# Sparse-attention loop of a hybrid decoder layer: filler weights' low parts by adding DMA, head outputs summed on VectorE, every key block in two float32r parts, masked 128-row compressed values

## The chip, the cores and the metric

One core of one Trainium2 chip runs the whole program. The metric is device time in microseconds (us) of one execution; lower is better. The time before is the median of three runs.

## What is computed

One decoder layer over 512 tokens of width 1024, in float32: a conditioned RMS norm, three token mixers side by side (a chunked gMLP, an mLSTM and NSA sparse attention), a gated merge, an output projection, a conditioned squared-ReLU MLP and a final norm. The change lies in the attention and in what runs beside it:

```python
sc = einsum('bgrqd,bgcd->bgrqc', qb, k_cmp) * scale - slopes * (tf - cmp_center)
p_c = masked_softmax(sc, cmp_end <= t);   o_cmp = einsum('bgrqc,bgcd->bgrqd', p_c, v_cmp)
o_sel = softmax over the selected blocks of 64 keys (8 of 8 here) @ v_sel
o_win = softmax over the last 512 keys @ v_win
out = gate_c * o_cmp + gate_s * o_sel + gate_w * o_win      # 8 heads of 64, in 2 groups of 4
```

There are 31 compressed positions a group. With 512 tokens the selected blocks are all blocks, so the second and the third branch are both full causal softmaxes, over different keys and values.

## The kernel before, in words

A product in float32 is made of float32r parts: hi is the value rounded to float32r, lo = value - hi, and a*b is hi*hi + hi*lo + lo*hi in PSUM. A function `split` (line 89 on) makes both parts: ScalarE copies the source to hi, then VectorE subtracts. `chunk` (line 105) does it for weights: SyncE loads 128x1024 into `w_raw`, ScalarE makes `w_hi` (L109), VectorE or, with `pool_lo`, GpSimd makes `w_lo` (L110).

The attention (us 114 to 266 of the profile) is a loop written out by hand, in whose order TensorE, ScalarE and VectorE are held. It has 18 steps n of four quarters i. Step n belongs to the pair (head h = n // 2, branch n % 2). A quarter holds, in this order:

- `scores(n, i)`: queries of 128-token block i times all keys up to it (PE L511, L512), then bias and row maximum in one VectorE pass (L513; L516 negates the four maxima after block 3);
- `exps(n-1, ..)`: ScalarE exponentials and row sums of the step before (L521);
- `turn(n-2, i)`: TensorE transposes (L541) of key block i, and their evacuation from PSUM to `pt`. In quarter 0 it comes behind the filler;
- `run(fill, ..)`: some six matmuls of the filler, which computes other projections of the layer (`early_fill`, 12 units of one chunk; L889, L905). At a unit's start it calls `chunk` for the next unit, with `pool_lo`;
- `apply(..)`, three quarters behind its `turn`: values times `pt` into the head's accumulator (L566), ahead of the filler in quarter 0. The first one of a head adds the compressed branch (L558, L559);
- `scale(n-1, ..)` in quarters 2 and 3: VectorE multiplies two rows of scores each by gate / sum (L527, L528, L531). The quarter-0 transposes of the next step need all four.

Key blocks 0 and 1 (512 and 384 query columns) are split into `pt_hi` and `pt_lo` against float32r values `V2` = [hi | lo]; blocks 2 and 3 (256 and 128 columns) stay float32: ScalarE copies them to `pt` (L548), and one float32 matmul multiplies them by `V32` = [v | 0], which runs as two instructions. The compressed values `vc` of a head are 32 of 128 rows; its matmul uses these 32 rows alone. The accumulator has 128 rows: 64 of the hi values, 64 of the lo values. When a head is done, in quarter 2 of the even steps 4 to 18, ScalarE copies both halves (L573); when the second head of a pair is done, GpSimd adds the halves and splits the sum (L581 to L583), and for the last pair VectorE and ScalarE do. GpSimd also makes a head's `bias` (L503) in this stretch. The second group's compressed scores (`cmp_scores(1)`) are worked off in pieces in steps 4 to 7.

Of the kernel before, what the change touches and what calls it, by code (L numbers as in the profile page):

```python
# [24 lines left out]
GELU_A = 0.044715  # L25
ML_SCALE = 128.0 ** -0.5
FILL_AT = (1, 2, 3, 4)
DVE_HI = False
SB_BUFS = 3
PRE_FILL = 16  # L30
LAST_X = (6,)
CONV_POOL = False
# [4 lines left out]
ADA_BUFS = 8  # L37
DVE_LO = ((1, 0), (1, 1), (1, 2), (1, 3))
CMP_AT = ((4, 0), (4, 2), (5, 0), (5, 2), (6, 0), (6, 2), (6, 3), (7, 1))
SPLIT_SB = (0,1)  # L40
SLOPES = [2.0 ** (-(h + 1)) for h in range(8)]


# [17 lines left out]
def trunk_kernel(ctx: ExitStack, tc: tile.TileContext, x, vecs, rows, late_rows, ada1, w_ada,  # L61
# [40 lines left out]
        nc.sync.dma_start(raw[:, :cols], src)  # L102
        return raw[:, :cols]

    def chunk(src, cols=D, pool_lo=False, dve_hi=False):
        raw = load(src, cols)
        hi = stream.tile([P, D], F32R, name="w_hi", tag="hi")[:, :cols]
        lo = stream.tile([P, D], F32R, name="w_lo", tag="lo")[:, :cols]
        V.tensor_copy(hi, raw) if dve_hi else A.copy(hi, raw)  # L109
        (G if pool_lo else V).tensor_tensor(lo, raw, f(hi), op=ALU.subtract)  # L110
        return hi, lo

    def mm3(ps, ah, al, bh, bl, first, last):
# [128 lines left out]
    with tc.manual_schedule(engines={mybir.EngineType.PE}):  # L242
# [6 lines left out]
        for j in range(KD):  # L249
# [7 lines left out]
            for i in range(6):  # L257
# [15 lines left out]
    G.memset(flag, 1.0)  # L273
    G.affine_select(out=flag, in_=flag, pattern=[[0, 1]], compare_op=ALU.is_ge, fill=0.0, base=-31,
                    channel_multiplier=1)
    dmask = const.tile([P, P], F32, name="dmask")
    G.memset(dmask, 0.0)
    G.affine_select(out=dmask, in_=dmask, pattern=[[1, P]], compare_op=ALU.is_ge, fill=-NEG, base=0,
# [104 lines left out]
    def compress(n):  # L383
        hp = bank("S", "hid")
        for m in range(16):
            T.matmul(hp[:, :128], phis[n][:, m].rearrange("p s c -> p (s c)"),
                     wins[n][:, m].rearrange("p s c -> p (s c)"), start=m == 0, stop=m == 15)
        hs = small.tile([64, 64], F32, name="c_hid")
        t1 = small.tile([64, 64], F32, name="c_t1")
        A.copy(t1, hp[64:128, :64])  # L390
        V.tensor_tensor(t1, t1, hp[:64, 64:128], op=ALU.add)
        V.tensor_tensor(hs, t1, hp[:64, :64], op=ALU.add)
        V.tensor_tensor(t1, hs, hs, op=ALU.mult)
        V.tensor_scalar(t1, t1, GELU_A, 1.0, op0=ALU.mult, op1=ALU.add)
        V.tensor_tensor(t1, t1, hs, op=ALU.mult)
        A.activation(t1, t1, AF.Tanh, scale=GELU_C)
        V.scalar_tensor_tensor(t1, t1, 1.0, hs, op0=ALU.add, op1=ALU.mult)
        V.tensor_scalar(hs, t1, 0.5, None, op0=ALU.mult)
        if n == 0:
            kp = bank("S", "kcmp")  # L400
            T.matmul(kp[:, :64], p2[:, 0:128], hs, start=True, stop=True)
            split(kc2[:, :, 0, :], kc2[:, :, 1, :], kp[:, :64].rearrange("p (g c) -> p g c", g=2))
            return
        for g in range(2):
            hr = small.tile([64, 4, 32], F32, name="c_rep")
            V.tensor_copy(hr, hs[:, g * 32:(g + 1) * 32].unsqueeze(1).to_broadcast([64, 4, 32]))
            vp = bank("S", "vcmp")
            T.matmul(vp[:, :64], hr.rearrange("e r c -> e (r c)"), p2[:, 128:192], start=True, stop=True)
            vv = nsa.tile([P, 128], F32R, name=f"vc{g}")
            split(vv[:, 0:64], vv[:, 64:128], vp[:, :64])  # L410
            vc.append(vv)

    windows(0, zt(ZT_NKC, True, "T"), V_PEK)
    windows(1, zt(ZT_NVC, True, "T"), V_PEV)
# [2 lines left out]


    V2 = [page("kv", f"v2_{tb}", F32R).rearrange("p (b g e) -> p b g e", b=2, g=2) for tb in range(NT)]
    V32 = [nsa.tile([P, 2, 2, 128], F32, name=f"v32_{tb}") for tb in range(NT)]  # L420
    mg = const.tile([P, NT, 8], F32, name="mg")
    gate = const.tile([P, NT, 24], F32, name="gate")
    gv3 = gate.rearrange("p t (h b) -> p t h b", b=3)
# [11 lines left out]
                T.matmul(sm[tb][:, :288], hh[k][:, tsl(tb)], wl[:, ws_], start=False, stop=k == KD - 1)  # L435
    for tb in range(NT):
        src = sm[tb][:, 0:256].rearrange("p (b g e) -> p b g e", b=2, g=2)
        V.tensor_copy(V32[tb][:, :, :, 0:64], src)
        G.memset(V32[tb][:, :, :, 64:128], 0.0)
        split(V2[tb][:, :, :, 0:64], V2[tb][:, :, :, 64:128], V32[tb][:, :, :, 0:64])  # L440
        V.tensor_tensor(mg[:, tb, :], sm[tb][:, 256:264], gb, op=ALU.add)
        A.activation(gate[:, tb, :], sm[tb][:, 264:288], AF.Tanh, scale=0.5)
    V.tensor_scalar(gate, gate, 1.0, 0.5, op0=ALU.add, op1=ALU.mult)
# [91 lines left out]
    def turn(n, sb):  # L535

        sb_ = step_[n][0]
        c0 = sb * P
        tp = bank("T", "pT")
        for tb in range(sb, NT):  # L540
            T.transpose(tp[:, tsl(tb)], sb_[:, boff(tb) + c0:boff(tb) + c0 + P], ident)  # L541
        if sb in SPLIT_SB:
            ph, pl = temp(att, "pt_hi", "pt", 8, F32R), temp(att, "pt_lo", "pt", 8, F32R)
            split(ph[:, c0:], pl[:, c0:], tp[:, c0:])
            pts_[n, sb] = (ph, pl)
        else:
            pt = temp(att, "pt", "pt", 8)
            A.copy(pt[:, c0:], tp[:, c0:])  # L548
            pts_[n, sb] = (pt,)

    def apply(n, sb):

        h, br = divmod(n, 2)
        g, r = divmod(h, 4)
        if br == 0 and sb == 0:
            pr = slice(r * 32, r * 32 + 32)
            accs[h] = bank("acc", "pv")
            T.matmul(accs[h], vc[g][pr, :], pc[g][0][pr, :], start=True, stop=False)  # L558
            T.matmul(accs[h], vc[g][pr, :], pc[g][1][pr, :], start=False, stop=False)  # L559
        acc = accs[h]  # L560
        c0 = sb * P
        last = br == 1 and sb == NT - 1
        t = pts_.pop((n, sb))
        vv = (V2 if len(t) == 2 else V32)[sb][:, br, g, :]
        for p_ in t:
            T.matmul(acc[:, c0:], vv, p_[:, c0:], start=False, stop=last and p_ is t[-1])  # L566
        if not last:
            return
        i = h // 2
        if h % 2 == 0:  # L570
            yraw[i] = [temp(att, "y_c", "y_c", 2) for _ in range(2)]
        for part, y in enumerate(yraw[i]):
            A.copy(y[(h % 2) * 64:(h % 2) * 64 + 64, :], acc[part * 64:part * 64 + 64, :])  # L573
        if h % 2 == 1:
            y, y2 = yraw[i]
            ych[i], ycl[i] = page("yc", "yc_hi", F32R), page("yc", "yc_lo", F32R)
            if i == 3:
                V.tensor_tensor(y, y, y2, op=ALU.add)
                split(ych[i], ycl[i], y)
                return  # L580
            G.tensor_tensor(y, y, y2, op=ALU.add)  # L581
            G.tensor_copy(ych[i], y)
            G.tensor_tensor(ycl[i], y, f(ych[i]), op=ALU.subtract)  # L583


    gvr = [None] * 4
# [285 lines left out]
    def early_fill():  # L872

        units = [("t", 0), ("t", 1), ("t", 2), ("t", 3)] + [("z", g) for g in range(4)] + [
            ("t", 4), ("t", 5), ("t", 6), ("t", 7)]

        def prep(u):
            return chunk(w_tok[u[1]] if u[0] == "t" else w_zt[ZT_GU + u[1]], D, True, DVE_HI)

        nxt = prep(units[0])  # L880
        for m, (kind, i) in enumerate(units):
            wh, wl = nxt
            if m + 1 < len(units):
                nxt = prep(units[m + 1])
            if kind == "z":
                ps = bank("mm", "zt")
                mms = [(wh, k, o) for k in range(KD) for o in (hh, hl)] + [(wl, k, hh) for k in range(KD)]
                for n_, (w_, k, o) in enumerate(mms):
                    T.matmul(ps, w_[:, tsl(k)], o[k], start=n_ == 0, stop=n_ == len(mms) - 1)  # L889
                    if n_ % 3 == 2 and n_ < len(mms) - 1:  # L890
                        yield
                gur[i] = page("mr", "gu")
                A.copy(gur[i], ps)
                yield
                continue
            n, c = divmod(i, 2)
            if c == 0:
                ps = [bank("mm", "ztok") for _ in range(2)]

            mms = [(tb, kk, a_, wh) for tb in range(NT) for kk in range(4) for a_ in (hh, hl)]  # L900
            mms += [(tb, kk, hh, wl) for tb in range(NT) for kk in range(4)]
            for n_, (tb, kk, a_, w_) in enumerate(mms):
                k = 4 * c + kk
                o = ps[tb // 2][:, (tb % 2) * 256:(tb % 2) * 256 + 256]
                T.matmul(o, a_[k][:, tsl(tb)], w_[:, kk * 256:(kk + 1) * 256],  # L905
                         start=k == 0 and tb % 2 == 0 and a_ is hh and w_ is wh,
                         stop=k == KD - 1 and tb % 2 == 1 and w_ is wl)
# [468 lines left out]
```

## Time and profile before

| | |
|---|---|
| median of 3 runs | 974.91 us (974.37 to 975.87) |
| the profiled execution | 973.78 us, span 972.0 us |
| TensorE busy | 932.9 us (96%), 4688 matmuls |
| VectorE busy | 618.3 us (64%) |
| ScalarE busy | 404.4 us (42%) |
| GpSimd busy | 194.8 us (20%) |
| DMA | 111.72 MB, 115 GB/s on average |

Matmuls are pipelined, so a row's duration is longer than what it takes from the next one; the distance from start to start is what it costs. A wait is put down to the instruction that came last. Line numbers before are those of the kernel above; in the order of the changed kernel they are its own.

### The profile page before, as it was taken

Reading aid. Unit: us, or ns where it says so; the run is one execution under the profiler, and the core shown is the slowest. Engines: PE = TensorE matmul, PEld = TensorE weight load, DVE = VectorE, ACT = ScalarE, POOL = GpSimd, SP = SyncE. Lnnn points to the kernel's source line nnn. Section 1 sums busy time; section 2 is a strip of 40 time slices with the busy share of each in tenths; the row PEclk is TensorE's granted clock in tenths of the full one; section 3 lists DMA queues with packets and bytes.
Section 4 is the critical chain, followed back from the end, with each engine's and each line's share of the span. In section 5 each row is a group of like instructions: output and inputs, shape, how many; then the busy total and the mean of one; then the engine's idle time right before and its main releaser. Section 6 shows DMA issues by size and latency. Waiting matters only on the chain.

```text
span 972.0 us, 12530 instructions
## 1 busy us (share of the span) xinstructions
PE 932.9 (96%) x4688; PEld 781.5 (80%) x4688; DVE 618.3 (64%) x1186; ACT 404.4 (42%) x789; POOL 194.8 (20%) x130
## 2 busy tenths in 40 slices
PE   8789998998999999999999998999999999999997
PEld 6568996797877888888988887988888888888886
DVE  5977688777389666656688889766424254442435
ACT  4355565665463434444243344544321223432221
POOL 5564442332344123123300003000000000000001
PEclk8799999998999999999999999999999999999999
DMA  8643310110132122222478872364332323223222
GB/s 307 217 132 100 101 45 22 44 45 22 53 112 75 65 86 93 82 87 87 155 237 262 296 255 85 90 183 130 96 99 90 106 89 107 87 89 106 87 87 88
DMA packets 36286, 111.72 MB, mean 115 GB/s; under 512 B 4160, under 2 KB 4352, under 8 KB 36224
## 3 DMA queue, kind: packets, MB, share of 16 engines
q1 hardware_dynamic: 36224, 110.91, 35.1%
q8 instruction: 37, 0.61, 0.3%
q14 instruction: 25, 0.20, 0.1%
HBM read 108.80 MB, written 2.10 MB: 114 GB/s over the span
## 4 chain that ended last, share of the span: by engine, by line
PE 81%; DVE 13%; DMA 2%; issue 2%; ACT 1%; POOL 0%; SPq 0%; POOLq 0%; ACTq 0%
PE tok L1106 7%; PE tok L1105 7%; PE tok L1104 7%; PE m L115 6%; PE m L114 6%; PE m L116 6%; PE zt L120 5%; PE zt L121 5%; PE zt L293 5%; PE ztok L905 4%; PE pv L566 2%; DMA ada_raw<-in_ada 2%; PE up L120 2%; PE up L121 2%; PE up L858 2%
## 5 line engine op out<-in xcount | busy, mean ns | idle before, releaser
L109 ACT CAST w_hi<-w_raw 128x1024 fp32r<-128x1024 f32 (+2 forms) x137 | 141.4, 1033 | 248.7 <-PE tok L1105 97.1
L110 DVE TENSOR_TENSOR w_lo<-w_raw,w_hi 128x1024 fp32r<-128x1024 f32 x84 | 107.4, 1279 | 164.2 <-ACT w_hi L109 157.2
L110 POOL TENSOR_TENSOR w_lo<-w_raw,w_hi 128x1024 fp32r<-128x1024 f32 (+3 forms) x53 | 126.5, 2388 | 252.4 <-ACT w_hi L109 149.7
L120 PE MATMUL zt<-h_hi,w_hi 128*128 128x512 f32 x272 | 107.8, 396 | 0.0
L121 PE MATMUL zt<-h_lo,w_hi 128*128 128x512 f32 x272 | 107.4, 395 | 0.0
L114 PE MATMUL m<-h_hi,w_hi 128*128 128x512 f32 (+1 forms) x272 | 103.8, 382 | 0.0
L115 PE MATMUL m<-h_lo,w_hi 128*128 128x512 f32 (+1 forms) x272 | 103.7, 381 | 0.0
L116 PE MATMUL m<-h_hi,w_lo 128*128 128x512 f32 (+1 forms) x272 | 103.4, 380 | 0.0
L1104 PE MATMUL tok<-w_hi,f_hi 128*128 128x512 f32 (+1 forms) x232 | 88.7, 382 | 0.0
L1105 PE MATMUL tok<-w_hi,f_lo 128*128 128x512 f32 (+1 forms) x232 | 88.7, 382 | 0.0
L1106 PE MATMUL tok<-w_lo,f_hi 128*128 128x512 f32 (+1 forms) x232 | 84.4, 382 | 0.0
L293 PE MATMUL zt<-h_hi,w_lo 128*128 128x512 f32 x272 | 70.1, 393 | 0.0
L1246 POOL TENSOR_TENSOR o_g<-x,gfin 128x512 f32<-128x512 f32 x1 | 1.3, 1293 | 310.7 <-DVE x L1150 310.7
L120 PEld LDWEIGHTS zt<-h_hi,w_hi 128*128 128x128 f32 x272 | 51.4, 189 | 10.8 <-ACT num_lo L787 0.4
L121 PEld LDWEIGHTS zt<-h_lo,w_hi 128*128 128x128 f32 x272 | 51.4, 189 | 10.4
L114 PEld LDWEIGHTS m<-h_hi,w_hi 128*128 128x128 f32 x272 | 51.0, 187 | 10.8
L115 PEld LDWEIGHTS m<-h_lo,w_hi 128*128 128x128 f32 x272 | 51.1, 188 | 10.6
L116 PEld LDWEIGHTS m<-h_hi,w_lo 128*128 128x128 f32 x272 | 51.1, 188 | 10.5
L293 PEld LDWEIGHTS zt<-h_hi,w_lo 128*128 128x128 f32 x272 | 50.8, 188 | 10.5
L1104 PEld LDWEIGHTS tok<-w_hi,f_hi 128*128 128x128 f32 x232 | 43.6, 188 | 8.5
L1105 PEld LDWEIGHTS tok<-w_hi,f_lo 128*128 128x128 f32 x232 | 43.6, 188 | 8.5
L1106 PEld LDWEIGHTS tok<-w_lo,f_hi 128*128 128x128 f32 x232 | 43.6, 188 | 8.4
(396 smaller groups left out, 2018.3 us busy)
## 6 DMA issues: line engine op xcount, KB each, us to landing
w_raw<-in_w_m SPq DMA_DIRECT2D x64, 512.0 KB, 3.5
w_raw<-in_w_zt SPq DMA_DIRECT2D x38, 512.0 KB, 3.4
ada_raw<-in_w_ada SPq DMA_DIRECT2D x24, 512.0 KB, 4.5
ada_raw<-in_ada SPq DMA_DIRECT2D x32, 256.0 KB, 4.7
w_raw<-in_w_tok SPq DMA_DIRECT2D x12, 512.0 KB, 3.3
w_raw<-in_w_up SPq DMA_DIRECT2D x12, 512.0 KB, 3.5
w_raw<-in_w_out SPq DMA_DIRECT2D x8, 512.0 KB, 4.5
w_raw<-in_w_ada SPq DMA_DIRECT2D x8, 512.0 KB, 3.8
```

The costliest lines, as they stand in the source:

```text
L109: V.tensor_copy(hi, raw) if dve_hi else A.copy(hi, raw)
L110: (G if pool_lo else V).tensor_tensor(lo, raw, f(hi), op=ALU.subtract)
L114: T.matmul(ps, ah, bh, start=first, stop=False)
L115: T.matmul(ps, ah, bl, start=False, stop=False)
L116: T.matmul(ps, al, bh, start=False, stop=last)
L120: T.matmul(ps, ah, bh, start=first, stop=False)
L121: T.matmul(ps, ah, bl, start=False, stop=False)
L293: T.matmul(ps, wl[:, tsl(k)], hh[k], start=False, stop=k == KD - 1)
L905: T.matmul(o, a_[k][:, tsl(tb)], w_[:, kk * 256:(kk + 1) * 256], start=k == 0 and tb % 2 == 0 and a_ is hh and w_ is wh, stop=k == KD - 1 ...
L1104: T.matmul(p_, ah_, wh, start=k == 0, stop=False)
L1105: T.matmul(p_, al_, wh, start=False, stop=False)
L1106: T.matmul(p_, ah_, wl, start=False, stop=k == 2 * n - 1)
```

## The change

Four parts.

1. The filler's low part: ScalarE writes -hi to `w_lo` and a DMA on GpSimd's queue adds the weights from memory to it, in place of GpSimd's subtraction. This holds for the 12 filler chunks alone.
2. Key blocks 2 and 3 are split like 0 and 1: a subtraction more on VectorE each, two float32r matmuls in place of a float32 one. `V32`, its copies and its zeroing go, and `pt` has 10 buffers (8 before).
3. A finished head: ScalarE copies the lower half, VectorE adds the upper half to it. A finished pair is split by ScalarE and VectorE, for all pairs.
4. The compressed values are stored four times, each with all rows but one head's 32 set to zero by a mask, and the matmul uses 128 rows.

```diff
-    def chunk(src, cols=D, pool_lo=False, dve_hi=False):
+    def chunk(src, cols=D, pool_lo=False, dve_hi=False, dma_lo=False):
         raw = load(src, cols)
...
         V.tensor_copy(hi, raw) if dve_hi else A.copy(hi, raw)
-        (G if pool_lo else V).tensor_tensor(lo, raw, f(hi), op=ALU.subtract)
+        if dma_lo:
+
+            A.activation(lo, f(hi), AF.Copy, scale=-1.0)
+            G.dma_start(lo, src, accum_op=ALU.add)
+        else:
+            (G if pool_lo else V).tensor_tensor(lo, raw, f(hi), op=ALU.subtract)
...
-            vv = nsa.tile([P, 128], F32R, name=f"vc{g}")
+            vv = small.tile([P, 128], F32R, name="vc")
             split(vv[:, 0:64], vv[:, 64:128], vp[:, :64])
-            vc.append(vv)
+            vm = nsa.tile([P, 4, 128], F32R, name=f"vc{g}")
+            for r in range(4):
+                V.tensor_scalar(vm[:, r, :], f(vv), headm[:, r:r + 1], None, op0=ALU.mult)
+            vc.append(vm)
...
-        V.tensor_copy(V32[tb][:, :, :, 0:64], src)
-        G.memset(V32[tb][:, :, :, 64:128], 0.0)
-        split(V2[tb][:, :, :, 0:64], V2[tb][:, :, :, 64:128], V32[tb][:, :, :, 0:64])
+        split(V2[tb][:, :, :, 0:64], V2[tb][:, :, :, 64:128], src)
...
-        if sb in SPLIT_SB:
-            ph, pl = temp(att, "pt_hi", "pt", 8, F32R), temp(att, "pt_lo", "pt", 8, F32R)
-            split(ph[:, c0:], pl[:, c0:], tp[:, c0:])
-            pts_[n, sb] = (ph, pl)
-        else:
-            pt = temp(att, "pt", "pt", 8)
-            A.copy(pt[:, c0:], tp[:, c0:])
-            pts_[n, sb] = (pt,)
+        ph, pl = temp(att, "pt_hi", "pt", PT_BUFS, F32R), temp(att, "pt_lo", "pt", PT_BUFS, F32R)
+        split(ph[:, c0:], pl[:, c0:], tp[:, c0:])
+        pts_[n, sb] = (ph, pl)
...
-            pr = slice(r * 32, r * 32 + 32)
             accs[h] = bank("acc", "pv")
-            T.matmul(accs[h], vc[g][pr, :], pc[g][0][pr, :], start=True, stop=False)
-            T.matmul(accs[h], vc[g][pr, :], pc[g][1][pr, :], start=False, stop=False)
+            T.matmul(accs[h], vc[g][:, r, :], pc[g][0], start=True, stop=False)
+            T.matmul(accs[h], vc[g][:, r, :], pc[g][1], start=False, stop=False)
...
-            yraw[i] = [temp(att, "y_c", "y_c", 2) for _ in range(2)]
-        for part, y in enumerate(yraw[i]):
-            A.copy(y[(h % 2) * 64:(h % 2) * 64 + 64, :], acc[part * 64:part * 64 + 64, :])
+            yraw[i] = temp(att, "y_c", "y_c", 2)
+        y, y2 = yraw[i], temp(att, "y_c2", "y_c2", 1)
+        A.copy(y2[0:64, :], acc[64:128, :])
+        V.tensor_tensor(y[(h % 2) * 64:(h % 2) * 64 + 64, :], acc[0:64, :], y2[0:64, :], op=ALU.add)
         if h % 2 == 1:
-            y, y2 = yraw[i]
             ych[i], ycl[i] = page("yc", "yc_hi", F32R), page("yc", "yc_lo", F32R)
-            if i == 3:
-                V.tensor_tensor(y, y, y2, op=ALU.add)
-                split(ych[i], ycl[i], y)
-                return
-            G.tensor_tensor(y, y, y2, op=ALU.add)
-            G.tensor_copy(ych[i], y)
-            G.tensor_tensor(ycl[i], y, f(ych[i]), op=ALU.subtract)
+            split(ych[i], ycl[i], y)
...
-            return chunk(w_tok[u[1]] if u[0] == "t" else w_zt[ZT_GU + u[1]], D, True, DVE_HI)
+            return chunk(w_tok[u[1]] if u[0] == "t" else w_zt[ZT_GU + u[1]], D, dma_lo=True)
```

VectorE, step 10, from the second to the last quarter: here a head, the second of its pair, is finished. Before:

```order
L95 TENSOR_TENSOR pt_lo<-pT,pt_hi 128x384
L513 ISA scores,mx<-S,bias 128x384
L513 ISA mx 128x1
L527 RECIPROCAL sums<-sums 128x2
L528 TENSOR_TENSOR sums<-sums,gate 128x2
L531 TENSOR_SCALAR scores<-scores,sums 128x128
L531 TENSOR_SCALAR scores<-scores,sums 128x256
L513 ISA scores,mx<-S,bias 128x512
```

The same place after the change:

```order
L94 TENSOR_TENSOR pt_lo<-pT,pt_hi 128x384
L522 ISA scores,mx<-S,bias 128x384
L522 ISA mx 128x1
L94 TENSOR_TENSOR pt_lo<-pT,pt_hi 128x256
L577 TENSOR_TENSOR y_c<-pv,y_c_2200 64x512
L94 TENSOR_TENSOR yc_lo<-y_c,yc_hi 128x512
L536 RECIPROCAL sums<-sums 128x2
L537 TENSOR_TENSOR sums<-sums,gate 128x2
L540 TENSOR_SCALAR scores<-scores,sums 128x128
L540 TENSOR_SCALAR scores<-scores,sums 128x256
L522 ISA scores,mx<-S,bias 128x512
```

Three VectorE passes now stand ahead of the scaling: the new low part, the head's sum (`y_c`) and the pair's low part (`yc_lo`).

ScalarE, step 14, quarters 2 and 3: a filler unit starts and the last but one pair is finished. Before:

```order
L521 ACTIVATE scores,sums<-scores,mx 128x512
L548 COPY pt<-pT 128x256
L109 CAST w_hi<-w_raw 128x1024
L573 COPY y_c<-pv 64x512 x2
L548 COPY pt<-pT 128x128
```

The same place after the change:

```order
L530 ACTIVATE scores,sums<-scores,mx 128x512
L93 CAST pt_hi<-pT 128x256
L108 CAST w_hi<-w_raw 128x1024
L111 ACTIVATE w_lo<-w_hi 128x1024
L576 COPY y_c_2649<-pv 64x512
L93 CAST yc_hi<-y_c 128x512
L93 CAST pt_hi<-pT 128x128
```

The filler's `w_lo` now stands on ScalarE between `w_hi` and the copy of the head's half, for which VectorE waits.

GpSimd's queue, from the last chunk ahead of the filler to the second half of the first filler units. Before:

```order
L110 TENSOR_TENSOR w_lo<-w_raw,w_hi 128x576
L110 TENSOR_TENSOR w_lo<-w_raw,w_hi 128x1024 x2
L503 TENSOR_SCALAR bias<-master 128x512 x2
L110 TENSOR_TENSOR w_lo<-w_raw,w_hi 128x1024 x2
L503 TENSOR_SCALAR bias<-master 128x512
```

The same place after the change:

```order
L114 TENSOR_TENSOR w_lo<-w_raw,w_hi 128x576
L112 DMA w_lo<-in_w_tok 128x1024
L512 TENSOR_SCALAR bias<-master 128x512 x2
L112 DMA w_lo<-in_w_tok 128x1024 x3
L512 TENSOR_SCALAR bias<-master 128x512
```

The subtractions are gone from the queue, and DMAs stand in their place; the biases remain.

## Rows read from the trace of the kernel before

**Rows 1.** Waits of PE, us 98 to 262: us in total, times, longest us.

```profile
PE pT L541 <- DVE scores L531: 7.5, 8, 2.7
```

**Rows 2.** Busy time by stretch: us, PE, PEld, DVE, ACT, POOL, PEclk, DMA share, GB/s.

```profile
228.00:238.60 10.60, 6.91 (x33) 6.08 (x32) 7.82 (x14) 4.46 (x13) 5.38 (x4) 0.70 0.15 51
```

**Rows 3.** Chain that ended last, in order of time: start us, us, what.

```profile
201.14 0.71 PE ztok L905 x6
```

**Rows 4.** Timeline of PE, steps 12 and 13: start us, us, engine, line, op.

```profile
208.42 0.59 PE L566 MATMUL pv<-pt,v 128*128 128x256 f32 x2
208.66 0.53 PE L511 MATMUL S<-khh,q 128*128 128x384 f32 x1
209.03 0.33 PE L512 MATMUL S<-kll,q 128*128 128x384 f32 x1
...
211.73 0.49 PE L558 MATMUL pv<-pch,vc 32*128 32x512 f32 x1
212.06 0.39 PE L559 MATMUL pv<-pcl,vc 32*128 32x512 f32 x1
212.38 0.50 PE L566 MATMUL pv<-pt_hi,v 128*128 128x512 f32 x1
212.72 0.39 PE L566 MATMUL pv<-pt_lo,v 128*128 128x512 f32 x1
```

**Rows 5.** Timeline of POOL: two of the filler's low parts.

```profile
153.71 2.40 POOL L110 TENSOR_TENSOR w_lo<-w_raw,w_hi 128x1024 fp32r<-128x1024 f32 x1 [12.24 <-ACT w_hi L109]
...
227.88 2.38 POOL L110 TENSOR_TENSOR w_lo<-w_raw,w_hi 128x1024 fp32r<-128x1024 f32 x1 [12.38 <-ACT w_hi L109]
```

**Rows 6.** Timeline of DVE: scaling and small passes, long and short ones.

```profile
153.89 2.57 DVE L531 TENSOR_SCALAR scores<-scores,sums 128x128 f32<-128x128 f32 x2
...
171.89 2.08 DVE L528 TENSOR_TENSOR sums<-sums,gate 128x2 f32<-128x2 f32 x1
...
203.39 0.16 DVE L528 TENSOR_TENSOR sums<-sums,gate 128x2 f32<-128x2 f32 x1
203.59 0.55 DVE L531 TENSOR_SCALAR scores<-scores,sums 128x128 f32<-128x128 f32 x2
...
220.48 0.82 DVE L531 TENSOR_SCALAR scores<-scores,sums 128x384 f32<-128x384 f32 x2
...
228.16 2.12 DVE L516 TENSOR_SCALAR mx<-mx 128x4 f32<-128x4 f32 x1
```

**Rows 7.** Timeline of PE: transposes that waited for the scaling.

```profile
158.30 0.33 PE L541 MATMUL pT<-ident,scores 128*128 128x128 f32 x1 [1.45 <-DVE scores L531]
...
168.15 0.72 PE L541 MATMUL pT<-ident,scores 128*128 128x128 f32 x2 [0.38 <-DVE scores L531]
...
176.38 0.33 PE L541 MATMUL pT<-ident,scores 128*128 128x128 f32 x1 [0.85 <-DVE scores L531]
...
232.42 0.48 PE L541 MATMUL pT<-ident,scores 128*128 128x128 f32 x1 [2.72 <-DVE scores L531]
```

**Rows 8.** Groups of DVE, us 98 to 262: busy us, mean ns, idle before.

```profile
L95 DVE TENSOR_TENSOR pt_lo<-pT,pt_hi 128x512 fp32r<-128x512 f32 x16 | 11.1, 691 | 25.7 <-ACT pt_hi L94 25.7
```

**Rows 9.** Timeline of ACT: head copies of steps 6 and 10, filler's cast of step 14.

```profile
163.29 1.17 ACT L573 COPY y_c<-pv 64x512 f32<-64x512 f32 x2 [1.18 <-PE pv L566]
...
195.54 1.17 ACT L573 COPY y_c<-pv 64x512 f32<-64x512 f32 x2 [0.49 <-PE pv L566]
...
226.69 1.05 ACT L109 CAST w_hi<-w_raw 128x1024 fp32r<-128x1024 f32 x1
```

**Rows 10.** Timeline of PE: transposes at the start of step 11.

```profile
199.97 0.60 PE L541 MATMUL pT<-ident,scores 128*128 128x128 f32 x4
```

**Rows 11.** Timeline of ACT, then of PE: the first filler chunk, made and used.

```profile
93.18 1.64 ACT L109 CAST w_hi<-w_raw 128x576 fp32r<-128x576 f32 x2
...
101.72 0.76 PE L905 MATMUL ztok<-w_lo,h_hi 128*128 128x256 f32 x5
```

**Rows 12.** DMA issues, us 98 to 262: KB each, us to landing.

```profile
w_raw<-in_w_tok SPq DMA_DIRECT2D x5, 512.0 KB, 3.2
```

More of the change, by code (lines that the diff above doesn't have):

```diff
@@ L27 @@
 FILL_AT = (1, 2, 3, 4)
-DVE_HI = False
 SB_BUFS = 3
+PT_BUFS = 10
 PRE_FILL = 16
@@ L39 @@
 CMP_AT = ((4, 0), (4, 2), (5, 0), (5, 2), (6, 0), (6, 2), (6, 3), (7, 1))
-SPLIT_SB = (0,1)
 SLOPES = [2.0 ** (-(h + 1)) for h in range(8)]
@@ L275, in trunk_kernel @@
                     channel_multiplier=1)
+    headm = nsa.tile([P, 4], F32, name="headm")
+    G.memset(headm, 0.0)
+    for r in range(4):
+        G.memset(headm[r * 32:r * 32 + 32, r:r + 1], 1.0)
     dmask = const.tile([P, P], F32, name="dmask")
@@ L408, in compress @@
             T.matmul(vp[:, :64], hr.rearrange("e r c -> e (r c)"), p2[:, 128:192], start=True, stop=True)
-            vv = nsa.tile([P, 128], F32R, name=f"vc{g}")
+            vv = small.tile([P, 128], F32R, name="vc")
             split(vv[:, 0:64], vv[:, 64:128], vp[:, :64])
-            vc.append(vv)
+            vm = nsa.tile([P, 4, 128], F32R, name=f"vc{g}")
+            for r in range(4):
+                V.tensor_scalar(vm[:, r, :], f(vv), headm[:, r:r + 1], None, op0=ALU.mult)
+            vc.append(vm)
     windows(0, zt(ZT_NKC, True, "T"), V_PEK)
@@ L419, in trunk_kernel @@
     V2 = [page("kv", f"v2_{tb}", F32R).rearrange("p (b g e) -> p b g e", b=2, g=2) for tb in range(NT)]
-    V32 = [nsa.tile([P, 2, 2, 128], F32, name=f"v32_{tb}") for tb in range(NT)]
     mg = const.tile([P, NT, 8], F32, name="mg")
@@ L563, in apply @@
         t = pts_.pop((n, sb))
-        vv = (V2 if len(t) == 2 else V32)[sb][:, br, g, :]
+        vv = V2[sb][:, br, g, :]
         for p_ in t:
```

## The prediction

> **What bounds the kernel now.** I read first who TensorE waits for in the attention loop, since the page has it busy 96% of the span and everything in the change lies in that loop. There is one entry of size: transposes wait for VectorE's scaling of the scores, 7.5 us in 8 waits [rows 1]. The rest of the loop is TensorE at its own rate, so work taken from TensorE counts there, and work put on VectorE or ScalarE counts only where it makes a transpose later.
>
> Why is VectorE late at those places? The timelines of GpSimd and VectorE side by side answer it. Two scalings that normally start and end within 0.55 us take 2.57, a 2x128 pass takes 2.08 where its like takes 0.16, and a pass over four columns takes 2.12 [rows 6]. The first and the last of the three stand beside a low part of the filler on GpSimd, which takes 2.4 [rows 5], and end with it. These are also the places where TensorE stands: 1.45 us at 158.30, 0.85 at 176.38, 2.72 at 232.42 [rows 7]. After the last one TensorE ran for a while at the lower of its two clock levels (1.2 instead of 2.4 GHz): the stretch from 228.0 to 238.6 has a mean granted clock of 0.70, and TensorE was idle for 10.60 - 6.91 = 3.7 us of it [rows 2].
>
> **The change part by part, in start-to-start times.**
>
> *Key block 2 (256 columns) in two float32r matmuls.* The float32 pair starts at 208.42, the next product at 208.66 and the one behind that at 209.03 [rows 4]: 0.61 us for the pair and a 384-column product. Six float32r matmuls of 256 columns take 0.71 [rows 3], or 0.118 each; so a float32r pair costs 0.24 and 384 columns 0.18, together 0.42. Gain 0.19 per step, 16 steps: **-3.1 us**.
>
> *Key block 3 (128 columns).* Two instructions before, two after. No row times that pair by itself; bounds are half the gain of the wider block either way, -0.1 to +0.1 a step. I take 0, as the same weights have to be loaded once per instruction either way, and keep 1.5 us on each side.
>
> *128-row compressed values.* The two 32-row products and the product after them start at 211.73, 212.06, 212.38, and the next one at 212.72 [rows 4]: 0.99 us for three times 512 columns, which at the rate above are 0.71. If it is the 32 rows that cost the rest, 0.28 for each of 8 heads: **-2.2 us**. From below nothing is gained. I take the gain, for float32r products of 512 columns on 128 rows are the rule in this loop. The eight masking passes stand on VectorE before the loop's first scores, when it waits; with the copies to `V32` gone they cost nothing.
>
> *The low part moved from GpSimd to ScalarE and a DMA.* What goes are the collisions above. At 158.30 the scaling loses 2.57 - 0.55 = 2.0 us, but new low parts for blocks 2 and 3 come ahead of it; by columns from 0.69 for 512 [rows 8] that is 0.35 + 0.2, with fixed parts about 0.6. Gain 1.4. At 176.38 it loses 2.08 - 0.16 = 1.9 and gets 0.6; the gain is 1.3. Together **-2.7 us**.
>
> *The head's sum on VectorE's path.* This is the part I weigh most. In quarter 2 of an even step VectorE now waits for the last product of the head, for ScalarE's copy (0.58, half of 1.17 [rows 9]) and adds (0.69, as the subtraction of as many columns [rows 8]), and only then scales. Behind it come scaling of two rows (0.16 twice and 0.55), the pass over block 3's scores (about 0.69), the new 128-column low part (0.25), and scaling of the other two (0.16 twice and 0.82) [rows 6]. Sum: 0.58 + 0.69 + 0.87 + 0.69 + 0.25 + 1.14 = 4.2, with gaps 4.3 us until TensorE can transpose. When a pair is done, ScalarE's cast and VectorE's low part come on top: 0.58 + 0.69, 5.6 us in all.
>
> How long does TensorE leave? In step 10 ScalarE's copy starts at 195.54 [rows 9] and the transposes at 199.97 [rows 10]; the fourth is due 0.33 later, and with the 0.3 saved in between the window is 4.5. Step 10 completes a pair: 5.6 - 4.5 = +1.1. Steps 4, 8 and 12 complete a single head; they have one portion of filler less (0.71 [rows 3]), so the window is 3.8 and each gets +0.5, together +1.5. Step 6 completes a pair, and 1.1 us of the second group's normalisation stands in the path too: 163.29 + 5.6 + 1.1 = 170.0, where the last transposes started by 168.15 + 0.36 [rows 7, 9]; with the clock gain ahead of it lost, +1.7.
>
> *Step 14* decides most. Here a filler unit starts, and ScalarE has `w_hi` from 226.69 on, 1.05 us [rows 9], then now `w_lo`, as long, and only then the head's copy: 226.69 + 2.1 = 228.8. Adding 5.6 gives 234.4. The stall of before, which came from the collision, ended about 233.9: 232.42, then one more wait of the transposes behind it [rows 7]. So the collision goes, and the pair's sum, late by ScalarE, takes its place: +0.8 with the TensorE work saved in between, and the low clock of [rows 2] stays. Sum for heads: 1.1 + 1.5 + 1.7 + 0.8 = **+5.1 us**.
>
> *The adding DMA.* The first filler chunk has the least time: its cast ends at 94.8 [rows 11], `w_lo` on ScalarE, behind a small copy, at some 96.1, and TensorE wants it at 101.72 [rows 11], 5.6 us later. All other chunks are made a unit ahead. No accumulating DMA and none from GpSimd's queue is in this trace. The nearest row is a plain load of the same size, 3.2 us to landing [rows 12]; the upper bound I take is four times that, 12.8. Below 5.6 it costs nothing, at 12.8 it costs 7.2. I take nothing, being nearer to the plain load. By the Trainium skill (DMA: Bandwidth & Descriptors, section Anatomy of one DMA, SWDGE path) a DMA of this queue takes 2.0 us plus its bytes at 436 GB/s, an estimate of 3.2 us for 512 KB, and the sum would be the same; no row here shows it.
>
> *Rest.* GpSimd's zeroing, the mask and the sums it loses are not waited for. ScalarE gets 12 times 1.05 and loses half the head copies; outside step 14 it has idle time before the transposes arrive.
>
> **Sum:** -3.1 - 2.2 - 2.7 + 5.1 = -2.9 us. On the profiled execution's 973.8 this is 970.9; that execution lies 1.1 under the median of the runs, so I predict **972.0**, with 969 to 975 as this case's own range from the bounds above. About 0.2% (2 us) is what a measurement can tell here.
>
> **Rivals.**
>
> *VectorE is simply freed* (chance 0.22). If ScalarE is on time in step 14, the stall and the low clock there go. From the forecast: -0.8 of the shift, -3.7 of idle time, and half of the some 5 us that TensorE worked at the low level, -2.5 [rows 2]: -2.9 - 7.0 = -9.9, 965.0. For it speak the collisions, which explain all large waits before; against it the order on ScalarE. By the Trainium skill (GPSIMD Engine Reference, section Key points) GpSimd's elementwise work contends with VectorE instructions in a 2-port mode or with two SBUF inputs, and removing it all would give this result. The trace agrees with the rule, as a four-column pass of 2.12 us beside a 2.38 us GpSimd pass shows [rows 5, 6]; the biases stay on GpSimd.
>
> *VectorE becomes the bound* (0.23), the slower side. It has 32 low parts more, and for each it waits in order for ScalarE's cast; the 16 existing ones for block 0 already idle 25.7 us, 1.6 each [rows 8], today in TensorE's shadow. If a quarter of that, 0.4 us, comes into each of the 12 steps that ran without a stall, that is 4.8, and a second drop of the clock after the 2.5 us stall of step 6 costs another 2.5: -2.9 + 7.3 = +4.4, 979.3. It decides from stalls of more than 8.0 us in all, where I sum 5.1.
>
> *The adding DMA is late* (0.07). Slower from 5.6 + 2.9 + 2, about 10.5 us; at the bound of 12.8 +4.3, 979.2.
>
> *Nothing comes through* (0.08): the saved TensorE work lies in steps whose end VectorE sets; 974.9.
>
> **The numbers.** The forecast has 0.40. It is faster by over 2 us in some two thirds of its cases. With the first rival that gives 0.27 + 0.22 + a little = 0.51 for faster. For the same: 0.11 of the forecast and 0.08 of nothing, 0.19. Slower: 0.02 + 0.23 + 0.07 less what falls within, 0.30. The range of 8 in 10 goes from 964 in the first rival to 979 in the others.
>
> **What would show it.** Right: key block 2's pair starts 0.24 us apart, the three products of a head's start 0.24 each; no VectorE pass of over 2 us in the loop; the largest wait of TensorE behind step 14, for the scaling, behind `w_lo` and the head's sum; a second after step 6. Wrong: TensorE waiting for the filler's low part (the DMA), no stall after step 14 (VectorE freed), or waits in most steps, for low parts or scaling (VectorE bound).

## The result, and the profile after

The changed kernel takes **980.75 us** (median of 4 runs, 979.11 to 981.47), the kernel before 974.64 beside it: a ratio of 1.0059 with an interval of 1.0045 to 1.0073. It is slower by 6 us (0.6%), where 972.0 was forecast; the time lies 5.75 us above the forecast's own range of 969 to 975 and 1.75 us above the wide one of 964 to 979, on the side of the rival in which VectorE becomes the bound (979.3). The profiled execution has a span of 979.0 us, 7.0 more than that of before.

Waits of TensorE from 98 to 275 us; the columns are us in total, times, the longest. Before, the scaling's 7.5 us [rows 1] were the only entry of more than 0.6 us.

```profile
PE pT L550 <- DVE scores L540: 9.1, 10, 3.2
PE cT L498 <- DVE cbias L494: 2.6, 1, 2.6
PE pT L550 <- DVE pt_lo L94: 2.3, 3, 0.8
PE ztok L902 <- ACT gate L451: 2.2, 1, 2.2
```

Three waits are new: 2.6 us for the second group's normalisation, 2.3 us of transposes for a low part of key block 0, and 2.2 us ahead of the loop. The work of TensorE itself got shorter, as the timeline of PE shows in step 12 (start us, us, engine, line, op):

```profile
216.12 0.28 PE L569 MATMUL pv<-pt_hi,v 128*128 128x256 f32 x1
216.24 0.28 PE L569 MATMUL pv<-pt_lo,v 128*128 128x256 f32 x1
216.36 0.34 PE L520 MATMUL S<-khh,q 128*128 128x384 f32 x1
216.54 0.33 PE L521 MATMUL S<-kll,q 128*128 128x384 f32 x1
...
219.15 0.40 PE L561 MATMUL pv<-pch,vc 128*128 128x512 f32 x1
219.39 0.40 PE L562 MATMUL pv<-pcl,vc 128*128 128x512 f32 x1
219.62 0.40 PE L569 MATMUL pv<-pt_hi,v 128*128 128x512 f32 x1
219.85 0.40 PE L569 MATMUL pv<-pt_lo,v 128*128 128x512 f32 x1
```

The pair of key block 2 and the product behind it take 216.54 - 216.12 = 0.42 us, where they took 0.61; the three products at a head's start take 0.70, where they took 0.99 [rows 4]. Both are as forecast, and so is key block 3's pair: with the product behind it 0.45 us, before (210.13 to 210.58) and after (217.65 to 218.10). So the loss is in waits, and in the granted clock. From 98 to 275 us the granted clock was half of the full one (1.2 instead of 2.4 GHz) in three stretches, where before it was in one of 6.9 us (columns as in [rows 2]):

```profile
102.20:105.60 3.40, 3.40 (x18) 3.40 (x18) 1.46 (x12) 2.38 (x4) 0.00 (x0) 0.50 1.01 237
170.50:173.90 3.40, 3.40 (x13) 3.02 (x13) 1.91 (x8) 2.45 (x8) 0.00 (x0) 0.50 0.00 0
238.80:245.60 6.80, 4.43 (x19) 3.93 (x20) 4.93 (x19) 3.25 (x10) 0.00 (x0) 0.50 0.41 76
```

The largest wait is again at the start of step 15. ScalarE's timeline, then VectorE's, TensorE's, and the stretch by engines (us, PE, PEld, DVE, ACT, POOL, PEclk, DMA share, GB/s):

```profile
234.09 0.36 ACT L93 CAST pt_hi<-pT 128x256 fp32r<-128x256 f32 x1
234.34 1.06 ACT L108 CAST w_hi<-w_raw 128x1024 fp32r<-128x1024 f32 x1
235.43 1.06 ACT L111 ACTIVATE w_lo<-w_hi 128x1024 fp32r<-128x1024 f32 x1
236.51 0.58 ACT L576 COPY y_c<-pv 64x512 f32<-64x512 f32 x1
```

```profile
234.48 0.42 DVE L94 TENSOR_TENSOR pt_lo<-pT,pt_hi 128x256 fp32r<-128x256 f32 x1 [0.17 <-ACT pt_hi L93]
237.13 0.68 DVE L577 TENSOR_TENSOR y_c<-pv,y_c 64x512 f32<-64x512 f32 x1 [2.22 <-ACT y_c L576]
238.50 0.69 DVE L94 TENSOR_TENSOR yc_lo<-y_c,yc_hi 128x512 fp32r<-128x512 f32 x1 [0.68 <-ACT yc_hi L93]
239.10 0.16 DVE L536 RECIPROCAL sums<-sums 128x2 f32<-128x2 f32 x1
```

```profile
239.93 0.66 PE L550 MATMUL pT<-ident,scores 128*128 128x128 f32 x2 [3.20 <-DVE scores L540]
```

```profile
235.30:246.50 11.20, 6.77 (x37) 6.01 (x36) 6.45 (x22) 6.19 (x16) 0.86 (x1) 0.70 0.44 96
```

VectorE waits 2.22 us for the copy behind `w_hi` and `w_lo`, and 0.68 for the pair's cast, before it may scale. TensorE's transposes come 3.20 us late, and the stretch runs at a mean granted clock of 0.70, as before [rows 2]. This is the mechanism that was forecast for step 14. No VectorE pass in the loop takes over 2 us, as forecast too; but TensorE waits for a scaling or a low part in nine of the loop's steps, which was the sign given for VectorE as the bound.

### The profile page after: what moved, and what is told of

The parts are those of the page before. It is cut to its first block, busy times and chain, and to the rows that moved or that the text cites. A ratio compares the mean times of both kernels' runs of the same rounds, so it can differ in the third digit from the quotient of the medians.

```text
span 979.0 us, 12573 instructions
## 1 busy us (share of the span) xinstructions
PE 931.4 (95%) x4688; PEld 782.8 (80%) x4688; DVE 616.3 (63%) x1232; ACT 412.0 (42%) x796; POOL 165.3 (17%) x122
## 4 chain that ended last, share of the span: by engine, by line
PE 76%; DVE 15%; ACT 4%; issue 2%; DMA 2%; SPq 0%; POOL 0%; POOLq 0%; ACTq 0%
PE tok L1101 6%; PE tok L1102 6%; PE tok L1103 6%; PE m L119 6%; PE m L118 6%; PE m L120 6%; PE zt L124 6%; PE zt L125 5%; PE zt L302 5%; PE ztok L902 4%; PE up L124 2%; PE up L125 2%; PE up L855 2%; DVE ada_raw L219 2%; PE pT L550 1%
## 5 line engine op out<-in xcount | busy, mean ns | idle before, releaser
L114 POOL TENSOR_TENSOR w_lo<-w_raw,w_hi 128x1024 fp32r<-128x1024 f32 (+3 forms) x41 | 97.7, 2383 | 200.4 <-ACT w_hi L108 97.4
L302 PEld LDWEIGHTS zt<-h_hi,w_lo 128*128 128x128 f32 x272 | 50.8, 188 | 10.6
L94 DVE TENSOR_TENSOR pt_lo<-pT,pt_hi 128x512 fp32r<-128x512 f32 (+1 forms) x64 | 31.2, 489 | 32.0 <-ACT pt_hi L93 31.8
```

The source lines that it names most:

```text
L302: T.matmul(ps, wl[:, tsl(k)], hh[k], start=False, stop=k == KD - 1)
```

## The experiments

Theories 1 and 2 were set up first. Theory 1: the added `w_lo` on ScalarE delays what TensorE waits for. Theory 2: VectorE's path is too long, by the head's sum and the low parts. The runs were taken in three groups, each beside its own runs of the kernel before (medians 974.61 for e1 to e4, 973.73 for e5 to e8, 974.65 for e9 to e12, 974.64 for the changed kernel). A run's distance from that median is taken where runs of different groups are compared. With intervals of 1.4 to 3 us to either side of a run, a difference of two runs holds to some 2 to 4 us.

**The parts one by one**

`e1_pool_lo`: the adding DMA undone.

```diff
-            return chunk(w_tok[u[1]] if u[0] == "t" else w_zt[ZT_GU + u[1]], D, dma_lo=True)
+            return chunk(w_tok[u[1]] if u[0] == "t" else w_zt[ZT_GU + u[1]], D, pool_lo=True)
```

> The changed kernel with the filler's low part back on GpSimd (no adding DMA, no -hi on ScalarE); the other three parts stay. Theory 1 (ScalarE's order: the added w_lo of 1.06 us stands ahead of work that TensorE waits for) expects the 2.2 us wait ahead of the loop, the three waits of the transposes for a low part (2.3 us in all) and about 1 us of the stall of step 15 to go: 980.7 - 5.5 = 975, or up to 978 if the collisions with GpSimd come back in full. Theory 2 (VectorE's path: the head's sum and 32 more low parts make the transposes late) expects no gain, 980 to 983, as those passes stay and the collisions return.

Measured: 982.69 us, ratio 1.0076 (1.0046 to 1.0105), within what theory 2 expected. The DMA as a whole is no cause of the loss; taking it away costs 2 us more, which is not clear of noise. The waits for a low part go, as theory 1 said, but those for the scaling rise from 9.1 to 13.7 us.

`e2_y_pool`: the head's end as before (the - and + of that part of the diff exchanged).

> The changed kernel with the head's end as before (two copies by ScalarE, sums and parts of a pair by GpSimd); the other three parts stay. Theory 1 expects that most of the loss stays, as the added w_lo stays on ScalarE: 977 to 980. Theory 2 expects the waits of the transposes for the scaling to go and the TensorE time saved (5.5 us) to come through: 974.6 - 5.5 + 2.3 for the wait ahead of the loop, 971 to 974.

Measured: 974.02 us, 0.9991 (0.9973 to 1.0009), the upper end of theory 2. The head's sum costs 6.7 us here (6.1 above before, and 0.6 below it without). The wait for the normalisation in step 6 is gone with it.

`e3_only_dma`: the adding DMA alone; the other three parts undone.

> Of the change only the adding DMA with -hi on ScalarE; key blocks 2 and 3 in float32, the head's end and the 32-row compressed product as before. Theory 1 expects it to be slower than before by itself: 974.6 + 2.3 ahead of the loop + some 2.3 in waits for a low part, less up to 2.7 for the collisions that go, 976 to 979. Theory 2 expects 972 to 975, the collisions gone and only the wait ahead of the loop to pay.

Measured: **965.76 us**, 0.9900 (0.9875 to 0.9926), 8.9 us less than before. Theory 1 has fallen, and theory 2 missed too, by 6 us: neither had put the collisions so high. Waits of TensorE, 98 to 275 us, and the stretch behind step 14:

```profile
PE ztok L914 <- DMA w_lo<-in_w_tok: 1.9, 1, 1.9
PE pT L550 <- DVE pt_lo L94: 0.8, 1, 0.8
PE pT L550 <- DVE scores L540: 0.4, 1, 0.4
...
```

```profile
224.90:236.10 11.20, 10.94 (x75) 9.84 (x74) 6.23 (x26) 7.86 (x21) 5.76 (x5) 1.00 0.42 95
```

Of 7.5 us of waits for the scaling 0.4 are left, and the clock stays at 1.00 (2.4 GHz): this is the rival in which VectorE is simply freed, and it comes through by this part alone.

`e4_only_pe`: the two parts that shorten TensorE's work (float32r parts, 128-row product), the others undone.

> Of the change only what shortens TensorE's work: all key blocks in two float32r parts and the 128-row compressed values; low parts of the filler on GpSimd and the head's end as before. Theory 1 expects nearly all of the 5.5 us saved to come through: 969 to 971. Theory 2 (32 more low parts on VectorE count) expects 972 to 976.

Measured: 977.22 us, 1.0017 (1.0001 to 1.0032): just slower, though TensorE has 5 us less to do, and above what either theory expected. VectorE, GpSimd and TensorE at the start of step 4 show one way:

```profile
137.37 2.30 DVE L525 TENSOR_SCALAR mx<-mx 128x4 f32<-128x4 f32 x1
139.59 0.28 DVE L94 TENSOR_TENSOR pt_lo<-pT,pt_hi 128x128 fp32r<-128x128 f32 x1
```

```profile
137.28 2.37 POOL L114 TENSOR_TENSOR w_lo<-w_raw,w_hi 128x1024 fp32r<-128x1024 f32 x1 [8.09 <-ACT w_hi L108]
```

```profile
140.87 0.33 PE L550 MATMUL pT<-ident,scores 128*128 128x128 f32 x1 [2.31 <-DVE scores L540]
```

GpSimd's subtraction now stands ahead of the bias and starts at 137.28, where it stood behind the bias before, at 139.04. So it meets VectorE's passes at the end of step 3: one over four columns takes 2.30 us and the scaling is late behind it and behind the low part; TensorE stands 2.31 us. So a change of order elsewhere moved the collision to another place.

`e5_dma_cmp`: the adding DMA and the 128-row product. `e6_dma_f32r`: the adding DMA and the float32r parts. In both the head's end is as before. By now theory 3 had taken the place of 1 and 2: the loss is made by VectorE passes that wait for ScalarE and stand ahead of the scaling in VectorE's order. Theory 4: it is their length that counts.

> Two parts of the change: the adding DMA and the 128-row compressed values; key blocks 2 and 3 in float32 and the head's end as before (to make room, the values of key blocks 0 and 1 are split straight from PSUM, as in the changed kernel). Theory 3 (the loss is made by VectorE passes that wait for ScalarE and stand ahead of the scaling; the masked product has none) expects the gain of the product on top of the DMA alone: 965.8 - 8 x 0.3 = 963.4, or up to 965 with the values' splitting. If the masked product were what costs, it is above 968.

> Two parts of the change: the adding DMA and all key blocks in two float32r parts; the compressed product on 32 rows and the head's end as before. Theory 3 expects nearly all of the loss of 8 us between the DMA alone (965.8) and the run with three parts (974.0) here, plus the 2.4 us that the masked product no longer saves: 975 to 977. If the masked product were what costs, 963 to 966.

Measured: e5 963.10 us, 0.9900 (0.9885 to 0.9915); e6 976.66, 1.0039 (1.0022 to 1.0056). Both lie close to where theory 3 put them. Against before, e3 is at -8.9 us, e5 at -10.6, e6 at +2.9 and e2 at -0.6. So the masked product saves 1.8 us (e5 and e3) or 3.5 (e2 and e6), neither clear of noise by itself, and the float32r parts **cost** 11.8 us beside the DMA (e6 and e3), or 10.0 with the product on top of each (e2 and e5). TensorE's waits for the scaling are back in e6:

```profile
PE pT L547 <- DVE scores L537: 7.6, 8, 2.6
```

**Order or load**

`e7_late_lo`: e2 with VectorE's low parts of key blocks 2 and 3 behind the scaling of their quarter; `late_` is emptied there.

```diff
-        split(ph[:, c0:], pl[:, c0:], tp[:, c0:])
+        A.copy(ph[:, c0:], tp[:, c0:])
+        late = lambda: V.tensor_tensor(pl[:, c0:], tp[:, c0:], f(ph[:, c0:]), op=ALU.subtract)
+        late_.append(late) if sb >= 2 else late()
...
                     scale(n - 1, 2 * i - 4, 2 * i - 2)
+                while late_:
+                    late_.pop(0)()
```

> The run with three parts (head's end as before, 974.0), with one thing moved: VectorE's low parts of key blocks 2 and 3 stand behind the scaling of their quarter instead of ahead of it. As many instructions of the same length. Theory 3 (order) expects the waits of the transposes for the scaling to go and most of the 5.5 us of saved TensorE time to come through: 962 to 968, of it 2 us for the wait ahead of the loop. Theory 4 (VectorE simply has 0.8 us more to do in each step) expects 972 to 975.

Measured: 966.31 us, 0.9935 (0.9910 to 0.9960): 7.4 us below before, where e2 is at 0.6, so 6.8 us less with the same instructions in the loop. Theory 3 holds, theory 4 has fallen for most of the loss.

Behind the loop TensorE's order is another one in e7 as well, so I set the loop apart: from its first score product to the last `pt_hi` product of 384 columns, 883 products in every run.

| run | loop, us | TensorE's waits in it, us | at half clock, us |
|---|---|---|---|
| before | 150.9 | 7.7 | 6.9 |
| change | 155.2 | 14.2 | 10.2 |
| e3 | 142.3 | 1.6 | 0 |
| e6 | 151.1 | 8.6 | 6.9 |
| e2 | 149.9 | 10.1 | 6.8 |
| e7 | 142.6 | 6.0 | 0 |

The loop itself is 7.3 us shorter in e7 than in e2; 4.1 of it are waits, and the rest goes with the half clock. At half clock a filler product of 256 columns takes 0.21 us from start to start, else 0.12. The profiled execution of e7 is the fastest of its four, so its clock may flatter. VectorE at the end of step 14, first in e2, then in e7:

```profile
231.18 0.17 DVE L525 TENSOR_SCALAR mx<-mx 128x4 f32<-128x4 f32 x1
232.78 0.29 DVE L94 TENSOR_TENSOR pt_lo<-pT,pt_hi 128x128 fp32r<-128x128 f32 x1 [1.43 <-ACT pt_hi L93]
...
233.18 0.65 DVE L537 TENSOR_TENSOR sums<-sums,gate 128x2 f32<-128x2 f32 x1
233.86 2.25 DVE L540 TENSOR_SCALAR scores<-scores,sums 128x384 f32<-128x384 f32 x2
```

```profile
226.31 0.16 DVE L537 TENSOR_TENSOR sums<-sums,gate 128x2 f32<-128x2 f32 x1
226.50 0.82 DVE L540 TENSOR_SCALAR scores<-scores,sums 128x384 f32<-128x384 f32 x2
227.90 0.29 DVE L553 TENSOR_TENSOR pt_lo<-pT,pt_hi 128x128 fp32r<-128x128 f32 x1 [0.58 <-ACT pt_hi L552]
```

In e2 a pass of 0.29 us holds the scaling back for 1.43, and the scaling then falls beside GpSimd's sums of the pair and takes 2.25 instead of 0.82. TensorE waits 3.01 us there; in e7 it doesn't wait for the scaling at that place. GpSimd's timeline in e2:

```profile
232.55 1.26 POOL L584 TENSOR_TENSOR y_c<-y_c 128x512 f32<-128x512 f32 x1
...
234.57 1.26 POOL L586 TENSOR_TENSOR yc_lo<-y_c,yc_hi 128x512 fp32r<-128x512 f32 x1
```

`e8_all_late`: the whole change, with e7's move, and a finished head's copy, sum and split behind the scaling of quarter 3.

> The whole change with two things moved on ScalarE and VectorE: the low parts of key blocks 2 and 3 stand behind the scaling of their quarter, and a finished head's copy, sum and split stand behind the scaling of quarter 3 instead of ahead of that of quarter 2. Theory 3 (order) expects it near the run with the low parts moved alone, within 3 us of it, 963 to 970. Theory 4 (load) expects 976 to 981, as all of the work stays on VectorE.

Measured: 972.12 us, 0.9977 (0.9961 to 0.9993). That is 7.7 us less than the change as it was, outside what theory 4 allowed, but 2 us more than theory 3's end and 5.8 more than e7: moved behind the scaling, the head's sum still costs nearly as much. A new wait is a part of it: in step 11 ScalarE has the pair's cast, then `w_hi` and `w_lo`, and only then the cast of key block 0, for whose bank the transposes wait.

```profile
201.66 0.62 ACT L93 CAST yc_hi<-y_c 128x512 fp32r<-128x512 f32 x1 [1.23 <-DVE y_c L583]
...
203.07 1.04 ACT L108 CAST w_hi<-w_raw 128x1024 fp32r<-128x1024 f32 x1
204.14 1.06 ACT L111 ACTIVATE w_lo<-w_hi 128x1024 fp32r<-128x1024 f32 x1
205.22 0.58 ACT L552 CAST pt_hi<-pT 128x512 fp32r<-128x512 f32 x1
```

```profile
206.59 0.69 PE L550 MATMUL pT<-ident,scores 128*128 128x128 f32 x2 [2.16 <-DVE pt_lo L553]
```

TensorE then runs at half clock from 206.5 to 209.9 us. No run took this wait away by itself, so how the 5.8 us divide is not shown.

**ScalarE's order**

`e9_gate_first`: the whole change, with the gate's activations written ahead of the splitting of the values.

```diff
     for tb in range(NT):
+        V.tensor_tensor(mg[:, tb, :], sm[tb][:, 256:264], gb, op=ALU.add)
+        A.activation(gate[:, tb, :], sm[tb][:, 264:288], AF.Tanh, scale=0.5)
+    for tb in range(NT):
         src = sm[tb][:, 0:256].rearrange("p (b g e) -> p b g e", b=2, g=2)
         split(V2[tb][:, :, :, 0:64], V2[tb][:, :, :, 64:128], src)
-        V.tensor_tensor(mg[:, tb, :], sm[tb][:, 256:264], gb, op=ALU.add)
-        A.activation(gate[:, tb, :], sm[tb][:, 264:288], AF.Tanh, scale=0.5)
```

`e10_lo_later`: the whole change, with ScalarE's -hi one portion of filler later.

```diff
-            A.activation(lo, f(hi), AF.Copy, scale=-1.0)
-            G.dma_start(lo, src, accum_op=ALU.add)
+            def low():
+                A.activation(lo, f(hi), AF.Copy, scale=-1.0)
+                G.dma_start(lo, src, accum_op=ALU.add)
+            lows.append(low)
...
         nxt = prep(units[0])
+        lows.pop()()
...
                 if n_ % 6 == 5:
                     yield
+                    if lows:
+                        lows.pop()()
```

> The whole change with one thing moved ahead of the loop: the gate's four activations and the mLSTM gates' sums are written ahead of the splitting of the values, so that the PSUM banks of the small projections are free before the first filler product. Theory 3 (the 2.2 us wait of the first filler product, and the lower clock after it, come from ScalarE's order: values and w_lo ahead of the gate) expects 2 to 3 us less than the changed kernel, 978 to 979. A rival, that this wait is hidden by the loads behind it, expects no difference, 980 to 981.

> The whole change with one thing moved: ScalarE's -hi for the filler's low part stands one portion of filler (about a quarter of a step) behind w_hi, instead of right behind it. Theory 1 (what remains of it: w_lo on ScalarE delays pt_hi and the head's copy) expects the two waits for a low part of 0.75 us and 1 us of the stall of step 15 to go, 1.5 to 4 us less, 976.5 to 979. If w_lo's place doesn't matter, 980 to 981.

Measured: e9 977.98 us, 1.0027 (1.0007 to 1.0047); e10 977.56, 1.0017 (0.9999 to 1.0036). Each move gives about 3 us against the change as it was, as expected, so ScalarE's order costs something at both places, though the DMA as a whole gains: theory 1 had the mechanism, but the sum of the part wrong. Ahead of the loop the stretch of the first filler unit is, in the changed kernel, in e9 and in e10:

```profile
101.20:108.60 7.40, 7.39 (x48) 7.29 (x48) 2.29 (x18) 4.41 (x9) 0.90 (x1) 0.77 0.74 168
```

```profile
99.40:106.90 7.50, 7.01 (x56) 6.81 (x57) 3.74 (x22) 6.30 (x12) 1.40 (x2) 1.00 0.95 209
```

```profile
101.00:108.40 7.40, 7.37 (x59) 7.17 (x60) 2.38 (x20) 5.69 (x12) 0.90 (x1) 1.00 0.82 199
```

After a wait of 2.2 us TensorE ran at a mean clock of 0.77 in the changed kernel and did 48 products. In e9, after one of 0.7, it did 56 at 1.00; but in e10, after the same wait of 2.2 us, it did 59 at 1.00 too. So the shorter wait of e9 is shown (0.5 of the 1.5 us comes back as a wait for the adding DMA), and that the clock hangs on it is not. The profiled execution of e9 is a long one (980.09 of 974.61 to 980.39 us), so its gain stands on the medians. In e10 the longest wait at step 15 is 2.1 instead of 3.2.

`e11_dma_cmp_order`: e5 with both moves. `e12_late_lo_order`: e7 with both moves.

> The kernel with the adding DMA and the masked 128-row product (963.1), with both moves: the gate first, and -hi one portion behind w_hi. Waits left there: 2.2 us ahead of the loop, 0.8 for a low part, 1.2 for scalings. If all come from ScalarE's order, 959 to 961; if they are only exchanged for others, 962.5 to 964.

> The kernel with three parts and the low parts of key blocks 2 and 3 behind the scaling (966.3), with both moves: the gate first, and -hi one portion behind w_hi. Theory 3 expects 961 to 963.5; for the two float32r parts to pay at all it has to lie below the kernel without them in this call (959 to 961 expected of that), and theory 3 expects that it doesn't, as the transposes of block 2 wait for a PSUM bank in every even step.

Measured: e11 **961.56 us**, 0.9858 (0.9836 to 0.9880), the fastest, between the two cases expected; e12 964.57, 0.9894 (0.9865 to 0.9923), 1 us above what was expected. So in the best order tried, the float32r parts of key blocks 2 and 3 still cost 3 us. One reason shows: in step 7 the low part of block 3 stands behind a lengthened scaling and holds the PSUM bank of the next transposes. In e7:

```profile
164.32 1.91 DVE L540 TENSOR_SCALAR scores<-scores,sums 128x384 f32<-128x384 f32 x2
166.15 0.28 DVE L553 TENSOR_TENSOR pt_lo<-pT,pt_hi 128x128 fp32r<-128x128 f32 x1
```

```profile
166.48 0.66 PE L550 MATMUL pT<-ident,scores 128*128 128x128 f32 x4 [1.95 <-DVE pt_lo L553]
```

The wait is 1.95 us in e12 too, where TensorE runs at half clock from 167.1 to 170.5 us behind it; in e5 and e11 step 7 has one of 0.75. The other reason that the expectation of e12 gives, transposes of block 2 waiting in every even step, does not hold in the trace: in e7 they start 0.17 to 0.18 us behind the last score product in ten of the steps 2 to 15, as in e5. In step 14 they do come later, 0.42 us for 0.23 (221.33, 221.75), when VectorE's low part of block 0 has ended (221.00 + 0.69).

## Why the prediction was wrong

| step | forecast | by the runs |
|---|---|---|
| key blocks 2 and 3 in float32r | -3.1 | +10.0 (e2 - e5); +11.8 (e6 - e3) |
| 128-row compressed values | -2.2 | -1.8 (e5 - e3); -3.5 (e2 - e6) |
| low part moved from GpSimd | -2.7 | -8.9 alone (e3); -3.2 beside parts 2 and 4 (e2 - e4); -2.0 beside all (change - e1) |
| the head's sum | +5.1 | +6.7 (change - e2); +5.5 without the DMA (e1 - e4) |
| sum | -2.9 | +6.1 (-8.9 - 1.8 + 10.0 + 6.7 = +6.0) |

The sum closes by construction, as it adds the parts in the order DMA, product, float32r parts, head's sum; in another order each part has another share. The errors of the first and the third row have opposite signs, so the total missed by less (8.75 us) than the first term alone (13.1): that it came no further off is luck.

**The step that failed is the first.** The duration of each product was right, 0.42 and 0.70 us as worked out. But the term counted TensorE's saving only. The new low parts of VectorE were priced by their length, 0.35 + 0.2 us, at the few places where the scaling was late, and taken as hidden in the twelve other steps. Each of them waits for ScalarE's cast, which stands behind exponentials and the filler's casts, and the scaling stands behind it on VectorE. Moving them behind the scaling, with not an instruction less, took 6.8 of the 10.0 us away (e7). By the loops of e3 and e6, 142.3 and 151.1 us, the waits that the parts bring are 7.0 us, with 6.9 us at half clock where e3 has none, less what TensorE saves. The price was in the text, as the rival in which VectorE becomes the bound: low parts that wait in order for ScalarE. It had a chance of 0.23 and a quarter of the 1.6 us that block 0's low parts idle [rows 8]. The wait itself was near: in e6 VectorE idles 8.7 us ahead of the low parts of block 2 and 2.2 ahead of those of block 3, 0.7 us a step. What the forecast lacked is what stands behind such a wait: the scaling, moved beside GpSimd's work, and TensorE's clock.

**"ScalarE has idle time before the transposes arrive"** was the second error, of some 3 us at each of two places (e9, e10; the second takes in 1.1 us of the stall of step 15, which was forecast). Ahead of the loop `w_lo` and four casts, now straight from PSUM, stand before the gate's activations, which hold the banks that the first filler product needs. Both count: without `w_lo` the wait is 1.3 us (e1, e4), and with `w_lo` but the values by way of `V32` there is none for the gate (e3). I read only the DMA's time there. In steps 2, 9 and 11 `w_hi` and `w_lo` stand before the cast of key block 0, and the transposes wait 0.8 us for its bank; e10 takes one of these three waits away.

**The collisions.** That they explain the large waits of before is shown by e3. Their size came near in the company of the other parts (-3.2 and -2.0 for -2.7), but not for the reason given: the stall behind step 14 stays in e2 too, which has no head's sum on VectorE, by the new low part behind `w_lo`. By itself the DMA gives 8.9, close to the 9.9 of the first rival. By the Trainium skill (GPSIMD Engine Reference, section Key points) GpSimd shares its SBUF interfaces with VectorE, whose instructions in a 2-port mode or with two SBUF inputs contend with it. The trace of e3 agrees, with the wait for the scaling down from 7.5 to 0.4 us.

**The head's sum** was right in mechanism and nearly in size. Step 14 went as told, with the clock at 0.70; but as e2 stalls there for 3.01 us without the sum, the sum adds only 0.2 us to that wait, and a longer time at half clock (6.8 us for 3.4). Step 6 was put at +1.7; between e2 and the change step 6 is longer by 11.86 - 9.09 = 2.8 us, from start to start of its first score products. It has the 2.56 us wait for the normalisation behind the pair's split. Step 8 is 1.6 us shorter, as 3.4 us at half clock follow the wait of step 6 in the changed kernel, and fall in step 8 in e2.

**The adding DMA** lands 5.6 us after its issue (median of 7 from `in_w_tok`, 98 to 262 us), where a plain load of the size takes 3.3; it lay within the bounds taken, above the value. The estimate of 3.2 us from the Trainium skill (DMA: Bandwidth & Descriptors, section Anatomy of one DMA, SWDGE path) is below what the trace shows. It matters at the first chunk alone: 1.9 us of wait in e3, none in the changed kernel, where TensorE is later anyway.

Left open: how much of the 3 us that the float32r parts cost in e12 is the bank, how much collisions with GpSimd's sums and biases, and how much the clock behind them; no run took these away alone.

## What to carry to other kernels

Price an added pass on an in-order engine by the wait for its input plus its length, and ask what stands behind it in that engine's order; a subtraction of 0.29 us held the scaling back by 1.43. Where a pass isn't needed for several stages, place it behind the one that the bounding engine waits for. And time the parts of a bundle apart: here two of four gave 10.6 us together (e5), and the other two took 16.7 back.

## What the runs showed of the hardware

Profiled executions differ ahead of all changed work: the last product of the small projections starts between 95.7 us (e5) and 98.9 (before), so spans of single executions compare only to some 3 us, and the medians carry the verdicts. A wait of TensorE did not settle its clock: ahead of the loop one of 2.2 us was followed by half the granted clock for 3.4 us in the changed kernel, e5 and e6, and by the full clock in e2, e7, e8 and e10. In step 7 one of 1.95 us was followed by half the clock in e12 and not in e7. After the longer ones, of 2.56 to 3.2 us in steps 6 and 15, products ran at half clock in every execution profiled.
